# A transformer layer with attention, gated DeltaNet and routed experts: front work moved between engines and queues, unread products on TensorE, router by blocks of 128 channels

## The chip, the cores and the metric

One core of a Trainium2 chip runs the whole layer. The metric is device time in microseconds, the median of the runs shown. Times inside the kernel are microseconds from the first instruction of one profiled execution.

## The reference, cut to what matters

One layer on 1024 latent and 256 context tokens of 1024 channels, float32. RMSNorm and modulation, one input projection (2832 columns), then two groups of heads: softmax attention (8 query heads, 2 key heads) and a gated DeltaNet (4 heads of 128, scanned in both directions). One output projection, a gated residual, and experts that choose their tokens:

```
h2 = modulate(rmsnorm(x, norm2_w), sh2, sc2)
affinity = softmax(h2 @ router_w)                      # 1024 x 16
gates, idx = top_k(affinity.T, 128)                    # 128 tokens for each of 16 experts
hid = silu(xg @ w_gate) * (xg @ w_up)                  # xg = h2[idx]
x = x + g2 * scatter_add(idx, (hid @ w_down) * gates)
```

## The kernel before, in words

Every large product is done in three passes of float32r halves (high times high, low times high, high times low), so each weight matrix is split into a high part (ScalarE copy) and a low part (a subtraction). A compiler orders each engine's instructions ahead of time from the program's order and its own estimates; each engine and each DMA queue then runs its list strictly in that order. `issue_after` puts an instruction behind a named one on its engine.

*Front, about 50 to 410 us.* `in_proj` (line 503) goes over eleven groups of columns. While group i is multiplied, `weights` (413) loads and splits group i+1: the subtraction (426) is on VectorE for the first groups and on GpSimd from the seventh on. Convolved channels (`conv_head`, `conv_tail`) go to DRAM as `skT` and `sqT`. Between the tiles of the later groups, `tick` runs pieces of the DeltaNet's preparation: `dn_chunk` (798) loads keys and queries of a chunk (`kq`, two loads) and a row of cumulated decays (`grow`), subtracts the decay of each row on GpSimd (808), takes Relu (814) and Exp (815) of 512 elements on ScalarE for two or three matrices E, multiplies keys by keys and queries on TensorE (825, 827), scales the products by E on VectorE (829 to 834) and masks them on GpSimd (843). `dn_wave` (848) inverts 32x32 blocks in 62 small VectorE instructions and stores the inverse and its transpose `sT`; the transposition (869) and both stores are on ScalarE and its queue. `rope_first` prepares keys with tiles of one buffer each (`sr_raw`, `sr_sp`), loads on SyncE (1027), stores on ScalarE's queue (1029). Queries (629) and the output gate (617) leave PSUM through `zz`, a tile with two buffers, whose store (626, 636) SyncE issues.

*Middle, about 410 to 880 us.* `att_open` (1041) loads the split keys (`ksplit`, 1052, SyncE; three loads through two slots) and transposes them (1056). Twenty `dn_step`s (949) and sixteen `att_group`s (1087) alternate. Each step loads eight small blocks of the inverse (896), the matrix N, keys, values, and `kT` and `qT` separately, all on SyncE. `att_q` (1064) prepares the next two query tiles when a group has hp == 2.

*Output and routing, about 860 to 978 us.* For each of eight token tiles: `out_norm`, `out_mm` (48 products of 512 columns in two halves of the row), and `out_route` (1289): eight transposes over channels with stride 8 (1300), two copies to SBUF (1301), eight narrow products with the router's weights (1305), a copy (1308), one more product (1315); one Square over the 1024 channels (1311), the inverse root in eleven tiny VectorE instructions, the logits (1318), the exponential (1320) and the scaled row `xn` (1324) that is stored for the experts' gather. `top_out` sorts and merges the tile's affinities on VectorE with a short product between (1402). After tile 7, line 237 takes the threshold, `route` (1452 to 1487) ranks the tokens, `expert_pick` (1500) makes the indices, and the gathered rows are transposed (1526).

*Experts, about 978 us to the end.* `expert_mm` streams 144 products of 512 columns an expert; a planner (`queue`) fixes every engine's order.

Of the kernel before, what the change touches and what calls it, by code (L numbers as in the profile page):

```python
# [32 lines left out]
P = 128  # L33
D = 1024
KT = 8
# [48 lines left out]
class Layer:  # L84
# [51 lines left out]
    def build(self):  # L136
# [13 lines left out]
        self.att_open()  # L150
        self.dn_open()
# [261 lines left out]
    def weights(self, col0, n, extra=None, eng=None):  # L413
# [6 lines left out]
        for k in range(0, KT, 4):  # L420
# [5 lines left out]
            (eng or nc.vector).tensor_tensor(lo[:, k:k + 4], raw, hi[:, k:k + 4], op=ALU.subtract)  # L426
# [76 lines left out]
    def in_proj(self, first):  # L503
# [4 lines left out]
        self.skT = self.dr.tile([NT, P, DH, P], F32, name="skT")  # L508
        self.sqT = self.dr.tile([NT, P, DH, P], F32, name="sqT")
# [48 lines left out]
        for i, (nm, c0, h, extra) in enumerate(groups):  # L558
            if i + 1 < len(groups):
                W.append(self.weights(groups[i + 1][1], 256, eng=nc.gpsimd if i > 5 else nc.vector))  # L560
# [34 lines left out]
        self.close("kp")  # L595
        self.close("pp")
# [20 lines left out]
    def out_gate(self, hi, lo, h2):  # L617
        nc = self.nc
        for t in range(NLAT):
            ps = self.bank("s")  # L620
            self.token_major(ps, t + NCTX, hi, lo, 0, 256)
            th = self.wp.tile([P, 256], F32, name="zt", bufs=1)
            nc.scalar.activation(th, ps[:, :256], AF.Tanh, scale=0.5)
            z = self.wp.tile([P, 256], F32, name="zz", bufs=2)
            nc.vector.scalar_tensor_tensor(z, th, 1.0, ps[:, :256], op0=ALU.add, op1=ALU.mult)  # L625
# [3 lines left out]
    def queries(self, hi, lo, g):  # L629
        nc = self.nc  # L630
        for t in range(NLAT):
            ps = self.bank("s")
            self.token_major(ps, t + NCTX, hi, lo, 0, 256)
            q = self.wp.tile([P, 256], F32, name="zz", bufs=2)
# [37 lines left out]
    def conv_tail(self, cp, name, h, acc, b0):  # L672
# [7 lines left out]
        if name != "v":  # L680
            st = self.sqT if name == "q" else self.skT
# [21 lines left out]
    def gates(self):  # L703
# [53 lines left out]
        v.tensor_copy(tot.rearrange("p c u -> p (c u)"), ps[:, 80:160])  # L757
        self.egc, self.ekd, self.egl = new("egc", k), new("ekd", k), new("egl", k)
# [39 lines left out]
    def dn_chunk(self, pp, c):  # L798
# [4 lines left out]
        nc.sync.dma_start(kq[:, :, 0], self.skT[c])  # L803
        if lat:
            nc.sync.dma_start(kq[:, :, 1], self.sqT[c])
        gr = pp.tile([P, 8, P], F32, name="grow", bufs=2)
        nc.sync.dma_start(gr.rearrange("p u j -> p (u j)"), dram(self.sgc, c * 8 * P, [[0, P], [1, 8 * P]]))
        nc.gpsimd.tensor_tensor(gr, gr, self.gc[:, c, :, None].to_broadcast([P, 8, P]), op=ALU.subtract)
        E = {}
        for key, d, sg in (("f", 0, 1.0), ("b", 1, -1.0), ("q", 0, -1.0)):  # L810
# [3 lines left out]
            nc.scalar.activation(e, gr[:, 4 * d:4 * d + 4], AF.Relu, scale=sg)  # L814
# [33 lines left out]
    def dn_wave(self, pp, w, units, v):  # L848
        nc = self.nc
        n = 16 * len(units)  # L850
        sT = self.dr.tile([2, P, 1024], F32, name=f"sT{w}")
# [17 lines left out]
        nc.scalar.copy(Tt[:n], T[:n].rearrange("p i j -> p j i"))  # L869
        nc.scalar.dma_start(sT[0, :n], T[:n].rearrange("p i j -> p (i j)"))  # L870
        nc.scalar.dma_start(sT[1, :n], Tt[:n].rearrange("p i j -> p (i j)"))


    def dn_open(self):
        nc = self.nc
        sp = self.sp = self.open("sp")
        self.F = [[sp.tile([P, DH, P], F32, name=f"F{d}{i}") for i in range(2)] for d in range(2)]
        self.X = [[sp.tile([P, DH, 64], F32, name=f"X{d}{i}") for i in range(2)] for d in range(2)]
        for d in range(2):
            for i in range(2):  # L880
                nc.gpsimd.memset(self.F[d][i], 0.0)
                nc.gpsimd.memset(self.X[d][i], 0.0)
# [3 lines left out]
    def dn_merge(self, sp, s, d, c):  # L886
        nc = self.nc
        F, X = self.F[d][s % 2], self.X[d][s % 2]
        sT, i = self.sT[c, d]
        base = i * 16 * 1024  # L890
        of, ox = (1, 0) if d == 0 else (0, 1)
        for b in range(4):
            pr = slice(32 * b, 32 * b + 32)
            cb = 32 * (b % 2)
            for dst, o in ((F[pr, :, 32 * b:32 * b + 32], of), (X[pr, :, cb:cb + 32], ox)):
                nc.sync.dma_start(dst, dram(sT, o * P * 1024 + base + b * 1024, [[32, 32], [4096, DH], [1, 32]]))
# [880 lines left out]
```

## Time and profile before

| | us |
|---|---|
| runs shown (three) | 1550.82, 1551.98, 1552.12; median 1551.98 |
| the profiled execution's own time | 1550.66 |
| its span, first to last instruction | 1548.9 |
| TensorE busy | 1443.1 |
| VectorE / ScalarE / GpSimd busy | 1178.0 / 949.0 / 222.8 |
| mean granted clock of TensorE | 0.967 |

Outside the span lie 1.8 us. [...]

### The profile page before, as it was taken

Reading aid. Unit: us, or ns where it says so; the run is one execution under the profiler, and the core shown is the slowest. Engines: PE = TensorE matmul, PEld = TensorE weight load, DVE = VectorE, ACT = ScalarE, POOL = GpSimd, SP = SyncE. Lnnn points to the kernel's source line nnn. Section 1 sums busy time; section 2 is a strip of 40 time slices with the busy share of each in tenths; the row PEclk is TensorE's granted clock in tenths of the full one; section 3 lists DMA queues with packets and bytes.
Section 4 is the critical chain, followed back from the end, with each engine's and each line's share of the span. In section 5 each row is a group of like instructions: output and inputs, shape, how many; then the busy total and the mean of one; then the engine's idle time right before and its main releaser. Section 6 shows DMA issues by size and latency. Waiting matters only on the chain.

```text
span 1548.9 us, 25613 instructions
## 1 busy us (share of the span) xinstructions
PE 1443.1 (93%) x9416; PEld 1173.8 (76%) x9416; DVE 1178.0 (76%) x2456; ACT 949.0 (61%) x1513; POOL 222.8 (14%) x230
## 2 busy tenths in 40 slices
PE   4899998997899999999899996799999999999997
PEld 1887787886777787788577664688888888888885
DVE  2825578698678686576574588899999999999996
ACT  2815455434285544566774543688888888888884
POOL 0000003423111121111400021111111111111101
PEclk7999999997999999999999998899999999999999
DMA  9356826777734456541342575889999999999992
GB/s 356 103 187 212 287 84 180 223 237 247 224 82 146 138 176 183 143 136 53 94 149 94 181 292 211 315 300 394 382 396 394 394 387 391 399 396 384 381 371 43
DMA packets 187048, 377.27 MB, mean 244 GB/s; under 512 B 47631, under 2 KB 124187, under 8 KB 159403
## 3 DMA queue, kind: packets, MB, share of 16 engines
q1 hardware_dynamic: 176320, 339.94, 61.9%
q0 software_dynamic: 7488, 29.36, 6.3%
q10 hardware_dynamic: 3115, 6.34, 1.1%
q8 instruction: 74, 1.21, 0.3%
q14 instruction: 51, 0.42, 0.1%
HBM read 321.91 MB, written 53.68 MB: 242 GB/s over the span
## 4 chain that ended last, share of the span: by engine, by line
PE 71%; DVE 12%; DMA 8%; ACT 5%; issue 2%; POOL 1%; SPq 1%; POOLq 0%; ACTq 0%; DVEq 0%
PE ps_m L1601 32%; PE ps_t L1129 4%; PE ps_a L1112 3%; PE ps_t L1122 3%; PE ps_s L441 3%; PE ps_s L443 3%; PE ps_s L442 3%; PE ps_t L1601 2%; PE ps_d L975 1%; DMA woraw<-in_w_out 1%; DMA sz<-zz 1%; PE ps_d L296 1%; PE ps_d L981 1%; PE ps_d L1284 1%; PE ps_d L1283 1%
## 5 line engine op out<-in xcount | busy, mean ns | idle before, releaser
L1601 PE MATMUL ps_m<-ehi,xx 128*128 128x512 f32 x1024 | 259.7, 396 | 0.4 <-DVE xx L1538 0.4
L1601 DVE TENSOR_TENSOR elo<-eraw,ehi 128x2048 fp32r<-128x2048 f32 x102 | 231.3, 2288 | 20.1 <-ACT ehi L1601 19.6
L1601 ACT ACTIVATE ehi<-eraw 128x2048 fp32r<-128x2048 f32 x105 | 201.3, 1918 | 54.7 <-PE ps_m L1601 45.4
L1601 PEld LDWEIGHTS ps_m<-ehi,xx 128*128 128x128 f32 x1024 | 189.9, 189 | 38.3 <-ACT xf L1534 0.8
L1601 PE MATMUL ps_m<-elo,xx 128*128 128x512 f32 x512 | 137.4, 390 | 0.0
L1601 PE MATMUL ps_m<-ehi,hx 128*128 128x512 f32 x512 | 129.7, 395 | 0.0
L1115 DVE TENSOR_SCALAR_CACHE_REDUCE prob<-ps_a 128x416 f32<-128x416 f32 (+1 forms) x192 | 109.4, 595 | 26.0 <-PE ps_a L1112 16.2
L1601 DVE TENSOR_TENSOR elo<-fraw,ehi 128x2048 fp32r<-128x2048 f32 x51 | 115.8, 2287 | 9.1 <-ACT ehi L1601 9.0
L1112 PE MATMUL ps_a<-kts,QT 128*128 128x416 f32 (+1 forms) x384 | 109.1, 390 | 4.0 <-DVE prob L1115 3.9
L1601 ACT ACTIVATE ehi<-fraw 128x2048 fp32r<-128x2048 f32 x51 | 97.8, 1917 | 24.2 <-PE ps_m L1601 21.4
L1601 PEld LDWEIGHTS ps_m<-elo,xx 128*128 128x128 f32 x512 | 96.3, 188 | 20.5
L1123 ACT ACTIVATE PT<-ps_t 128x512 f32<-128x512 f32 (+1 forms) x192 | 93.7, 525 | 28.8 <-PE ps_t L1122 26.9
L1601 PEld LDWEIGHTS ps_m<-ehi,hx 128*128 128x128 f32 x512 | 94.0, 188 | 18.2
L1122 PE MATMUL ps_t<-consts,prob 128*128 128x128 f32 x640 | 100.2, 282 | 3.1 <-ACT PT L1123 1.7
L433 PE MATMUL ps_s<-whi,hh 128*128 128x256 f32 (+1 forms) x336 | 98.0, 293 | 3.9 <-DVE zz L625 2.1
L1745 POOL DMA_INDIRECT out_x<-ey,idx x16 | 52.0, 3252 | 342.3 <-DVE ey L1601 342.3
L1118 ACT ACTIVATE prob<-prob,mn 128x1280 f32<-128x1280 f32 x64 | 87.2, 1363 | 19.1 <-DVE mn L1117 18.4
L435 PE MATMUL ps_s<-whi,hl 128*128 128x256 f32 (+1 forms) x336 | 95.8, 289 | 0.9 <-DVE hl L410 0.9
L434 PE MATMUL ps_s<-wlo,hh 128*128 128x256 f32 (+1 forms) x336 | 95.5, 287 | 0.0
L441 PE MATMUL ps_s<-hh,whi 128*128 128x512 f32 (+1 forms) x256 | 95.1, 372 | 0.0
L443 PE MATMUL ps_s<-hh,wlo 128*128 128x512 f32 (+1 forms) x256 | 94.3, 368 | 0.0
L442 PE MATMUL ps_s<-hl,whi 128*128 128x512 f32 (+1 forms) x256 | 94.0, 367 | 0.0
(434 smaller groups left out, 3134.5 us busy)
## 6 DMA issues: line engine op xcount, KB each, us to landing
eraw<-in_w_up SPq DMA_DIRECT2D x38, 1024.0 KB, 9.4
eraw<-in_w_down SPq DMA_DIRECT2D x32, 1024.0 KB, 7.0
eraw<-in_w_gate SPq DMA_DIRECT2D x31, 1024.0 KB, 8.8
wmod<-in_w_mod SPq DMA_DIRECT2D x24, 1024.0 KB, 6.3
fraw<-in_w_down SPq DMA_DIRECT2D x21, 1024.0 KB, 7.6
fraw<-in_w_gate SPq DMA_DIRECT2D x16, 1024.0 KB, 9.8
fqraw<-in_w_gate SPq DMA_DIRECT2D x16, 1024.0 KB, 9.7
fraw<-in_w_up SPq DMA_DIRECT2D x14, 1024.0 KB, 8.4
```

The source lines that it names most:

```text
L433: self.nc.tensor.matmul(ps[:, :n], self.hh[:, k, ts], hi[:, k, a:a + n], start=st, stop=False)
L434: self.nc.tensor.matmul(ps[:, :n], self.hh[:, k, ts], lo[:, k, a:a + n], start=False, stop=False)
L435: self.nc.tensor.matmul(ps[:, :n], self.hl[:, k, ts], hi[:, k, a:a + n], start=False, stop=en)
L441: self.nc.tensor.matmul(ps[:, :n], hi[:, k, a:a + P], self.hh[:, k, ts], start=st, stop=False)
L442: self.nc.tensor.matmul(ps[:, :n], hi[:, k, a:a + P], self.hl[:, k, ts], start=False, stop=False)
L443: self.nc.tensor.matmul(ps[:, :n], lo[:, k, a:a + P], self.hh[:, k, ts], start=False, stop=en)
L1112: nc.tensor.matmul(ps[:, k0:min(k0 + 512, w)], QT[:, h, i], self.KTs[:, kv * 2 + x, ks], start=x == 0, stop=x == 1)
L1115: v.tensor_scalar(pr[:, c0:c0 + w], ps[:, :w], -1.0, 3e38, op0=ALU.mult, op1=ALU.min, accum_out=mn[:, y:y + 1])
L1118: nc.scalar.activation(pr, pr, AF.Exp, bias=mn[:, 3:4], scale=-1.0, accum_out=rs[:, a, hp, i:i + 1])
L1122: nc.tensor.transpose(pt[:, x * P:(x + 1) * P], pr[:, (k0 + x) * P:(k0 + x + 1) * P], self.ident)
L1123: nc.scalar.activation(PT[g][:, :, a, i], pt[:, :n * P].rearrange("p (x q) -> p x q", x=n), AF.Copy)
L1601: i = fn(*args, **kw)
```

## The change

It has four groups of edits. (1) **Front:** the weight split is always on VectorE; the decay of the row is added inside ScalarE's Relu, head by head (four of 128 in place of one of 512), so the GpSimd subtraction is gone; `skT` and `sqT` become one array `skq` with one load in place of two, in `dn_chunk` and in `dn_step`; `zz` has four buffers in a pool of its own and the tanh is done in place; the router's loads are issued at the first query group and its constants are made before the last gate group; the inverse and its transpose are stored from SyncE, the transposition is on VectorE; the eight block loads of a step become four. (2) **Attention's start:** the first query tile is prepared before the DeltaNet's tiles are opened, the next ones at hp == 1; `ksplit` and the first query tile are loaded from GpSimd's queue, and the third key load has a slot of its own. (3) **Router:** transposes take contiguous blocks of 128 channels (the router's weights are re-laid through DRAM), the square is taken per half row between them, and the row copy is tied behind the exponential. (4) **Unread products:** 18 products of 512 columns in bfloat16 behind tile 7's product of line 1402, and 10 behind the second `expert_pick`; nothing reads them.

```diff
@@ build, in_proj, weights
         self.att_open()
+        self.att_q(0)
         self.dn_open()
-            (eng or nc.vector).tensor_tensor(lo[:, k:k + 4], raw, hi[:, k:k + 4], op=ALU.subtract)
+            nc.vector.tensor_tensor(lo[:, k:k + 4], raw, hi[:, k:k + 4], op=ALU.subtract)
...
+                self.zp = self.open("zp")
+                self.router_loads(self.wp)
...
-                self.out_gate(hi, lo, h)
                 if h:
                     self.router_consts(self.wp)
+                self.out_gate(hi, lo, h)
@@ out_gate (queries alike)
-            z = self.wp.tile([P, 256], F32, name="zz", bufs=2)
+            z = self.zp.tile([P, 256], F32, name="zz", bufs=4)
@@ dn_chunk
-        nc.sync.dma_start(kq[:, :, 0], self.skT[c])
-        if lat:
-            nc.sync.dma_start(kq[:, :, 1], self.sqT[c])
+        nc.sync.dma_start(kq if lat else kq[:, :, 0], self.skq[c] if lat else self.skq[c, :, :, 0])
...
-        nc.gpsimd.tensor_tensor(gr, gr, self.gc[:, c, :, None].to_broadcast([P, 8, P]), op=ALU.subtract)
...
-            nc.scalar.activation(e, gr[:, 4 * d:4 * d + 4], AF.Relu, scale=sg)
+            off = self.ngc if sg > 0 else self.gc
+            for h in range(DH):
+                u = 4 * d + h
+                nc.scalar.activation(e[:, h], gr[:, u], AF.Relu, bias=off[:, c, u:u + 1], scale=sg)
@@ dn_wave
-        nc.scalar.copy(Tt[:n], T[:n].rearrange("p i j -> p j i"))
-        nc.scalar.dma_start(sT[0, :n], T[:n].rearrange("p i j -> p (i j)"))
-        nc.scalar.dma_start(sT[1, :n], Tt[:n].rearrange("p i j -> p (i j)"))
+        nc.sync.dma_start(sT[:, 0].rearrange("g (b r) -> g b r", b=4), T[:n].rearrange("p i j -> p (i j)"))
+        v.tensor_copy(Tt[:n], T[:n].rearrange("p i j -> p j i"))
+        nc.sync.dma_start(sT[:, 1].rearrange("g (b r) -> g b r", b=4), Tt[:n].rearrange("p i j -> p (i j)"))
@@ dn_merge
-            for dst, o in ((F[pr, :, 32 * b:32 * b + 32], of), (X[pr, :, cb:cb + 32], ox)):
-                nc.sync.dma_start(dst, dram(sT, o * P * 1024 + base + b * 1024, [[32, 32], [4096, DH], [1, 32]]))
+            nc.sync.dma_start(FX[32 * b:32 * b + 32, :, 32 * b:32 * b + 32], dram(sT, base + b * 1024, [[32, 32], [4096, 2 * DH], [1, 32]]))
@@ att_open, att_group
-            s = tp.tile([P, 2048], F32, name="ksplit", tag="PT4", bufs=2)[:, :512 * T]
+            s = (tw if T == 2 else tp).tile([P, 512 * T], F32, name="ksplit", tag=f"PT{T}", bufs=2)
-            nc.sync.dma_start(s, self.sks[t0:t0 + T].rearrange("t p i d -> p t i d"))
+            nc.gpsimd.dma_start(s, self.sks[t0:t0 + T].rearrange("t p i d -> p t i d"))
...
-        if hp == 2 and j < 3:
+        if hp == 1 and j < 3:
@@ out_route
-                nc.tensor.transpose(pt[:, i * P:(i + 1) * P], xv[:, 4 * g + i], self.ident)
+                nc.tensor.transpose(pt[:, i * P:(i + 1) * P], x1[:, (4 * g + i) * P:(4 * g + i + 1) * P], self.ident)
+
+            nc.scalar.activation(junk, x1[:, 512 * g:512 * g + 512], AF.Square, scale=D ** -0.5, accum_out=ss[:, g:g + 1])
...
-        nc.scalar.activation(junk, x1, AF.Square, accum_out=ss)
-        v.tensor_scalar(ss, ss, 1.0 / D, EPS, op0=ALU.mult, op1=ALU.add)
+        v.tensor_scalar(ms, ss[:, 0:1], ss[:, 1:2], EPS, op0=ALU.add, op1=ALU.add)
...
-        nc.scalar.activation(xn, x1, AF.Copy, scale=r2)
+        with self.tc.issue_after(ex.ins):
+            nc.scalar.activation(xn, x1, AF.Copy, scale=r2)
@@ top_out, experts
+            if t == NLAT - 1:
+                self.spin("d", 18, listed)
...
+    def spin(self, tag, n, behind):
+        ps = self.bank(tag)
+        with self.tc.issue_after(behind.ins):
+            for _ in range(n):
+                last = self.nc.tensor.matmul(ps, self.oneb, self.info.rearrange("p t e c -> p (t e c)")[:, :512], start=True, stop=True)
...
+        self.spin("m", 10, self.picked)
```

## Rows read from the trace of the kernel before

**Rows 1.** The profile's page: busy us, share of the span and instructions of each engine (PEld: weight loads of TensorE).

```profile
PE 1443.1 (93%) x9416; PEld 1173.8 (76%) x9416; DVE 1178.0 (76%) x2456; ACT 949.0 (61%) x1513; POOL 222.8 (14%) x230
```

**Rows 2.** The table of windows, whole core: the window, its length, then busy us (and instructions) of TensorE, its weight loads, VectorE, ScalarE and GpSimd, then TensorE's granted clock as a share of full speed, the DMA engines' busy share and GB/s.

```profile
240.00:280.00 40.00, 34.53 (x183) 29.04 (x182) 34.53 (x52) 20.28 (x36) 20.46 (x15) 0.96 0.80 233
...
320.00:360.00 40.00, 27.02 (x216) 25.73 (x214) 38.01 (x104) 15.83 (x26) 17.07 (x9) 0.84 0.72 230
...
400.00:440.00 40.00, 35.11 (x279) 31.54 (x277) 25.65 (x82) 21.94 (x45) 7.68 (x13) 0.91 0.75 203
600.00:640.00 40.00, 35.03 (x331) 30.21 (x330) 27.21 (x79) 19.72 (x43) 8.56 (x8) 0.87 0.59 176
```

**Rows 3.** What TensorE waited for between 225 and 425 us: engine, tile and line that waited, what ended the wait, us in total, times, longest.

```profile
PE ps_d L827 <- DVE Eb L834: 4.3, 1, 4.3
...
PE ps_a L1056 <- DVE rbias L1208: 2.7, 1, 2.7
PE ps_s L433 <- DVE zz L625: 2.1, 2, 1.1
PE ps_s L433 <- ACT zz L635: 1.8, 1, 1.8
```

**Rows 4.** Groups of instructions by line and shape: count, busy us, mean ns, idle before. The first is VectorE between 100 and 225 us (GpSimd free), the second the same line between 225 and 420 us.

```profile
L661 DVE SCALAR_TENSOR_TENSOR cacc<-craw,cw,cacc 128x1284 f32<-128x1284 f32 x16 | 24.9, 1556 | 0.7
...
L661 DVE SCALAR_TENSOR_TENSOR cacc<-craw,cw,cacc 128x1284 f32<-128x1284 f32 x16 | 28.3, 1769 | 0.4
```

**Rows 5.** The same view, GpSimd between 225 and 420 us; and the lines of the weight split by engine (ns min/median/max, first and last start).

```profile
L808 POOL TENSOR_TENSOR grow<-grow,g_gc 128x1024 f32<-128x1024 f32 x10 | 20.4, 2038 | 34.4 <-DMA grow<-sgc 34.4
L426 POOL TENSOR_TENSOR wlo<-wraw,whi 128x1024 fp32r<-128x1024 f32 x8 | 20.0, 2506 | 44.1 <-ACT whi L425 38.2 <-PE ps_t L690 6.0
...
L426 DVE TENSOR_TENSOR wlo<-wraw,whi x14: 1217/1222/1294, 34.8 to 210.3; 128x1024 fp32r<-128x1024 f32 x12, 128x1088 fp32r<-128x1088 f32 x2
```

**Rows 6.** ScalarE: the decay activation on 512 elements, a 128-element activation without a pointer operand (both 225 to 420 us), and one whose bias and scale are both per-partition pointers (min/median/max ns).

```profile
L814 ACT ACTIVATE Ef<-grow 128x512 f32<-128x512 f32 x10 | 6.3, 628 | 18.6 <-DVE rs_i L126 6.5 <-POOL grow L808 6.1 <-DMA sN<-Ef 3.1
L695 ACT ACTIVATE cjunk<-ps_t 128x128 bf16<-128x128 f32 x6 | 1.7, 278 | 0.2
...
L1534 ACT ACTIVATE xf<-ps_t,sh,a x4: 450/457/457, 976.9 to 979.5; 128x128 f32<-128x128 f32 x4
```

**Rows 7.** What the DMA queue of SyncE waited for between 225 and 420 us (columns as in rows 3).

```profile
SPq L769 <- DVE g_ckb L784: 20.4, 1, 20.4
SPq L626 <- DVE zz L625: 13.6, 7, 5.0
```

**Rows 8.** The largest stall, in order of time: a transfer from the chain of waits (start, us), an issue of SyncE's queue, and TensorE's next two products with the idle time before them.

```profile
339.76 8.68 DMA sks<-sr_sp
...
351.29 0.37 SPq L1027 DMA_DIRECT2D sr_raw<-skr  x1
...
356.15 2.04 PE L825 MATMUL ps_d<-kq 128*128 128x256 f32 x4 [11.18 <-issue]
361.47 2.04 PE L825 MATMUL ps_d<-kq 128*128 128x256 f32 x4 [3.27 <-DVE rs_a L130]
```

**Rows 9.** SyncE's queue before the opening of attention, in order of time (a row of two stores spans the time between them).

```profile
403.57 3.93 SPq L626 DMA_DIRECT2D sz<-zz  x2
407.59 0.39 SPq L1052 DMA_DIRECT2D ksplit<-sks  x1
```

**Rows 10.** What TensorE waited for between 880 and 985 us (columns as in rows 3).

```profile
PE ps_r L1315 <- ACT lg L1308: 1.8, 2, 1.4
PE ps_r L1305 <- ACT xT L1301: 1.5, 2, 0.9
```

**Rows 11.** Tile 7, ScalarE in order of time: square, row copy, exponential.

```profile
950.20 1.06 ACT L1311 ACTIVATE j<-xres 128x1024 bf16<-128x1024 f32 x1 [9.20 <-issue]
...
953.91 1.15 ACT L1324 ACTIVATE xn<-xres,rs_r 128x1024 f32<-128x1024 f32 x1 [0.71 <-DVE rs_r L132]
954.97 0.29 ACT L1320 ACTIVATE aff<-logit,mx 128x16 f32<-128x16 f32 x1
```

**Rows 12.** Before and at the start of the experts, windows of 5 us (columns as in rows 2).

```profile
955.00:960.00 5.00, 0.92 (x16) 0.69 (x16) 4.32 (x35) 4.06 (x5) 1.73 (x6) 0.50 0.99 410
960.00:965.00 5.00, 0.00 (x0) 0.00 (x0) 4.97 (x38) 1.91 (x1) 0.00 (x0) 0.50 1.02 428
...
980.00:985.00 5.00, 5.00 (x19) 3.96 (x17) 3.90 (x8) 1.92 (x1) 0.62 (x1) 0.77 1.02 429
```

**Rows 13.** TensorE there, in order of time, with the idle time before a group and what ended it.

```profile
958.56 0.59 PE L1402 MATMUL ps_l<-srt,consts 128*16 128x32 f32 x8 [2.19 <-DVE j1x L1347]
965.54 0.61 PE L1452 MATMUL ps_m<-consts,m 16*128 16x16 f32 x2 [6.39 <-DVE m L237]
...
972.06 0.37 PE L1500 MATMUL ps_t<-info,oh 128*128 128x5 bf16 x8 [1.55 <-DVE oh L1493]
976.21 1.97 PE L1526 MATMUL ps_t<-consts,xg 128*128 128x128 f32 x8 [3.77 <-DMA xg<-h,idx]
978.62 3.75 PE L1601 MATMUL ps_m<-ehi,xx 128*128 128x512 f32 x8 [0.43 <-DVE xx L1538]
...
983.16 2.00 PE L1601 MATMUL ps_m<-ehi,xx 128*128 128x512 f32 x8
...
985.90 1.98 PE L1601 MATMUL ps_m<-ehi,xx 128*128 128x512 f32 x8
```

More of the change, by code (lines that the diff above doesn't have):

```diff
@@ L559, in in_proj @@
             if i + 1 < len(groups):
-                W.append(self.weights(groups[i + 1][1], 256, eng=nc.gpsimd if i > 5 else nc.vector))
+                W.append(self.weights(groups[i + 1][1], 256))
             hi, lo = W.pop(0)
@@ L595, in in_proj @@
         self.close("kp")
+        self.close("zp")
         self.close("pp")
@@ L621, in out_gate @@
             self.token_major(ps, t + NCTX, hi, lo, 0, 256)
-            th = self.wp.tile([P, 256], F32, name="zt", bufs=1)
-            nc.scalar.activation(th, ps[:, :256], AF.Tanh, scale=0.5)
-            z = self.wp.tile([P, 256], F32, name="zz", bufs=2)
-            nc.vector.scalar_tensor_tensor(z, th, 1.0, ps[:, :256], op0=ALU.add, op1=ALU.mult)
+            z = self.zp.tile([P, 256], F32, name="zz", bufs=4)
+            nc.scalar.activation(z, ps[:, :256], AF.Tanh, scale=0.5)
+            nc.vector.scalar_tensor_tensor(z, z, 1.0, ps[:, :256], op0=ALU.add, op1=ALU.mult)
             nc.sync.dma_start(self.sz[t, :, h2:h2 + 2, :], z.rearrange("p (h d) -> p h d", h=2))
@@ L757, in gates @@
         v.tensor_copy(tot.rearrange("p c u -> p (c u)"), ps[:, 80:160])
+        self.ngc = new("ngc", k)
+        v.tensor_scalar(self.ngc, self.gc, -1.0, None, op0=ALU.mult)
         self.egc, self.ekd, self.egl = new("egc", k), new("ekd", k), new("egl", k)
@@ L876, in dn_open @@
         sp = self.sp = self.open("sp")
-        self.F = [[sp.tile([P, DH, P], F32, name=f"F{d}{i}") for i in range(2)] for d in range(2)]
-        self.X = [[sp.tile([P, DH, 64], F32, name=f"X{d}{i}") for i in range(2)] for d in range(2)]
+        self.FX = [[sp.tile([P, 2 * DH, P], F32, name=f"F{d}{i}") for i in range(2)] for d in range(2)]
         for d in range(2):
             for i in range(2):
-                nc.gpsimd.memset(self.F[d][i], 0.0)
-                nc.gpsimd.memset(self.X[d][i], 0.0)
+                nc.gpsimd.memset(self.FX[d][i], 0.0)
         self.so = [[self.dr.tile([P, DH, P], F32, name=f"so{d}_{t}") for t in range(NLAT)] for d in range(2)]
@@ L1189, in router_consts @@
         nc.sync.dma_start(m[:, 4], self.col(A["norm2_w"], 0))
+        rw = pool.tile([P, KT, NE], F32, name="rw")
+        nc.sync.dma_start(rw, dram(A["router_w"], 0, [[KT * NE, P], [1, KT * NE]]).rearrange("p (k e) -> p k e", k=KT))
+        self.router = m, rw
+    def router_consts(self, pool):
+        nc, k = self.nc, self.keep
+        v = nc.vector
+        m, rw = self.router
         self.sh2 = k.tile([P, KT], F32, name="sh2")
@@ L1295, in out_route @@
         xT = wo.tile([P, KT, P], F32, name="xT", bufs=1)
-        xv = x1.rearrange("p (q k) -> p k q", k=KT)
+        ss = wo.tile([P, 2], F32, name="ss2", bufs=2)
+        junk = wo.tile([P, 512], BF, name="j2", bufs=1)
         for g in range(2):
@@ L1319, in out_route @@
         v.tensor_reduce(mx[:, 0:1], lo, axis=AX.X, op=ALU.max, negate=True)
-        nc.scalar.activation(self.aff[:, t], lo, AF.Exp, bias=mx[:, 0:1], accum_out=mx[:, 1:2])
+        ex = nc.scalar.activation(self.aff[:, t], lo, AF.Exp, bias=mx[:, 0:1], accum_out=mx[:, 1:2])
         v.reciprocal(mx[:, 1:2], mx[:, 1:2])
```

66 lines of the change are left out of this document (30 added, 36 removed).

## The prediction

> **What bounds the kernel now.** The page comes first: TensorE is busy 1443.1 us of a span of 1548.9 and every other engine is far below it [rows 1], so time comes back where TensorE stands still or runs at its lower clock ahead of the experts; behind 978 us it streams products. The table of windows shows where: idle 5.5 us in 240 to 280, 13.0 in 320 to 360, 4.9 in 400 to 440, 5.0 in 600 to 640, with clocks of 0.84 to 0.96 [rows 2]. [...] The waits of TensorE and of SyncE's queue then say what ended each gap. In the front it is three things: VectorE late with the matrices E, the two-buffered zz, and SyncE's queue standing behind a wait [rows 3, 7, 8]. In the tail it is a chain of small VectorE and ScalarE instructions, behind which TensorE starts the experts cold [rows 10 to 13].
>
> **The change part by part.** The sum goes against the profiled execution's own 1550.66 us; the median of the runs shown, 1551.98, stands 1.3 above it and gets the same difference.
>
> *GpSimd's front work.* 20.4 us of row subtraction and 20.0 of weight split leave GpSimd [rows 5]. While GpSimd runs, VectorE is slow: line 661 takes 1556 ns a piece with GpSimd free and 1769 on average beside it, 3.4 us over 16 [rows 4]. The split comes back to VectorE as 8 pieces of 1.22 us, 9.8 us [rows 5], and the transposition of the inverse comes as well. So VectorE's total hardly falls; what falls is the path to E, which loses one subtraction of 2.04 us and a turn in GpSimd's list. The wait that this path ends is 4.3 us [rows 3]; two split pieces may stand before the products there (2.4 us). Bounds: -4.3 less the clock behind it (0.96 in that window, 3.2 us at half speed, 1.6 lost), so -5.9, to +2.4 if VectorE is simply later. I take **-3.5**, near the lower end, as the row waited for is E itself.
>
> *Relu head by head.* One activation of 512 elements is 628 ns [rows 6]. Four of 128 are between 4 x 0.278 = 1.11 us (no pointer operand) and 4 x 0.455 = 1.82 (two pointers) [rows 6]; the new one has one pointer. 28 matrices E make +13.5 to +33 us of ScalarE, which is busy 15.8 to 21.9 of 40 us there [rows 2], so most of it lies beside other work. [...] Exposed I take **+1.5** (0 to +15).
>
> *zz with four buffers.* TensorE waited 2.1 + 1.8 us for a bank that waited for zz, and SyncE's list stood 13.6 us for the gate's part of it alone [rows 3, 7]. Two more buffers cover a store of some 4 us. **-3.9** (0 to -3.9); late next is ScalarE's evacuation itself.
>
> *Attention's start.* The first transposition waited 2.7 us for the router's bias [rows 3], which is now made a group of columns earlier. The key load stood behind two output-gate stores for 3.9 us on SyncE [rows 9] and now goes on GpSimd's list, free there. [...] I take **-4.5** for waits and clock together (0 to -6.6, 2.7 + 3.9; the near end if the load is late anyway). [...]
>
> *The large stall.* From 344.98 to 361.47 TensorE does four products: SyncE's list stood at the load of sr_raw until 351.29, since VectorE waited for sr_sp, whose store took 8.68 us; kq came behind it [rows 8]. The change leaves sr_raw, sr_sp and that store as they are. Two waits, 11.18 + 3.27, and the slow clock (0.84, 12.8 us at half speed, mostly idle) make -17.5 the far end; the near end is 0. kq is one load instead of two, VectorE is disturbed less, and the second wait ended at a VectorE line. **-3.0**.
>
> *Stores of the inverse on SyncE, steps with fewer loads, att_q earlier.* ScalarE loses a copy a wave; each step issues five loads less. But the stores wait for VectorE's last instruction of a wave, and behind them in SyncE's list stand the next step's loads. The gap in 600 to 640 (5.0 us, clock 0.87, some 10 us at half speed) falls where att_q(2) and two steps meet; it can go or move. Bounds -10 to +40 (a rival below); I take **-1.0**.
>
> *Router.* TensorE waited 1.8 + 1.5 us for the copies of the logits and of the transposed row [rows 10]. The first half of a row can be transposed and squared before the second is there, and the Square of 1.06 us no longer stands before both copies [rows 11]. Two accumulator reads instead of one add some 0.2 us. **-2.5** (0 to -5). For tile 7 the exponential waited 0.94 us behind the row copy (953.91 to 954.97) [rows 11], but VectorE is busy 4.3 and 5.0 of each 5 us behind it [rows 12], so only its 0.7 us of idle can be won: **-0.7**. The router's weights through DRAM are ready hundreds of us early: 0.
>
> *Unread products.* TensorE is at half clock from 955 to about 982.3 (0.77 over 980 to 985 means 2.3 us slow) [rows 12]. The first twelve expert products took 983.16 - 978.62 = 4.54 us, the next twelve 985.90 - 983.16 = 2.74 [rows 13]; so a product is 0.23 us at full and 0.46 at half speed. 18 of them need 4.1 to 8.2 us; the room between lines 1402 and 1452 is 965.54 - 959.15 = 6.4 us [rows 13]. From 978.62 the first group of eight (3.75 us) went by before the clock rose [rows 12, 13]; eight slow and ten fast ones take 6.0 us: they just fit. The second ten (2.3 to 4.6 us) lie in the 3.7 us between 972.43 and the gathered rows at 976.21 [rows 13]. Won: 1.8 us on the first products and about 1.0 on ranks and transposes at half speed. **-2.8** (-3.5 to +1.8 if the block stays slow and delays line 1452).
>
> Sum: -3.5 + 1.5 - 3.9 - 4.5 - 3.0 - 1.0 - 2.5 - 0.7 - 2.8 = -20.4 us; 1550.66 becomes 1530.3, and the median 1531.6.
>
> **The rivals.** *The front gives it back.* The lists are in order, and SyncE, ScalarE and VectorE take on each other's work; if the front's gaps only move, zz, the router and the unread products remain: -3.9 - 2.5 - 0.7 - 2.8 = -9.9, 1542. For it: VectorE is busy 38.0 of 40 us in 320 to 360 [rows 2]. Against: 40 us of GpSimd work are gone.
>
> *The large stall goes too.* With another order of SyncE's list kq is loaded before sr_raw, and -3.0 becomes -17.5: 1517. For it: the order is made anew. Against: the same loads with the same single buffers.
>
> *Slower: SyncE held at the inverse's stores.* SyncE's list has stood 20.4 us for a VectorE result at line 769 [rows 7]. If the two later waves hold it as long in the middle of the scan, the steps' loads come late and TensorE, in order, stands: 2 x 20.4 = +40.8 on the sum, 1572. It decides from about 10 us a wave, where the gain is eaten. Against: twenty steps with five loads less leave that list slack, and attention groups lie between.
>
> *The unread products don't raise the clock.* Then -2.8 is 0 to +1.8, some 1535, inside the forecast's own range.
>
> **How the numbers follow.** Forecast 0.50 (with its own range, 1523 to 1539), gives back 0.23, stall gone too 0.16, held stores 0.11, of which 0.08 end slower and 0.03 near no change. Chances: faster 0.89, same 0.03, slower 0.08, by 0.2%, 3.1 us, about what a measurement of this kernel can tell from no change. The range 1511 to 1549 takes the first three cases with their spread and leaves out the held stores.
>
> **What would show it.** Right: no wait of line 433 for zz; no wait for the bias at line 1056; line 661 near 1556 ns in the front; the clock at full level at the first expert products, and twelve of them in 2.7 us; line 1452 not later behind line 1402 than 6.4 us. The stall at line 825 shows by its idle time which of the first three cases it is. Wrong: TensorE idle behind 420 us at lines 896 to 1009 while SyncE's list waits for the transposed inverse; the second row of products delaying the transposes of line 1526; or ScalarE full between 240 and 400 us, with products waiting for E.

## The result: 10 us faster, half of the forecast

| | median us | runs | range | ratio to before, 95% interval |
|---|---|---|---|---|
| before | 1552.05 | 10 | 1549.85 to 1559.29 | 1 |
| after | 1542.9 | 10 | 1539.5 to 1547.53 | 0.9933 [0.9915, 0.9951] |

The profiled execution took 1540.66 us, span 1538.9, against 1550.66 and 1548.9 before. Forecast were 1531.6 and a gain of 20.4. The milestones of the profiles (starts, us) say where the forecast parts from the run; the last column is an experiment told below.

| milestone | before | after | difference | early merge |
|---|---|---|---|---|
| end of the projection's products | 408.1 | 389.8 | -18.3 | 392.5 |
| first transposition of keys | 411.2 | 399.2 | -12.0 | 400.6 |
| first product of attention | 422.0 | 410.9 | -11.1 | 412.5 |
| last attention group copied out | 871.3 | 854.8 | -16.4 | 855.1 |
| tile 7: copy of the logits | 952.9 | 937.8 | -15.1 | 938.3 |
| tile 7: copy of its lists | 959.2 | 946.6 | -12.6 | 944.9 |
| reduction to the threshold | 965.2 | 957.0 | -8.2 | 950.5 |
| first expert product | 978.6 | 970.3 | -8.3 | 963.3 |
| 13th expert product | 983.2 | 973.2 | -10.0 | 966.1 |
| end of the span | 1548.9 | 1538.9 | -10.0 | 1532.0 |

So in these two profiles the front won 16.4 us where its terms summed to 14.4. From there to the threshold 8.2 were lost where 3.2 were to be won, and the unread products won 1.8. The 16.4 comes from one execution of each kernel: in seven profiles with this front the last attention group is copied out between 854.5 and 862.4 us, a gain of 8.9 to 16.7.

### The profile page after: what moved, and what is told of

Read it like the earlier page. It is cut to its first block, busy times and chain, and to the rows that moved or that the text cites. A ratio compares the mean times of both kernels' runs of the same rounds, so it can differ in the third digit from the quotient of the medians.

```text
span 1538.9 us, 25604 instructions
## 1 busy us (share of the span) xinstructions
PE 1448.0 (94%) x9442; PEld 1178.5 (77%) x9444; DVE 1170.9 (76%) x2468; ACT 961.1 (62%) x1610; POOL 187.6 (12%) x214
## 4 chain that ended last, share of the span: by engine, by line
PE 59%; DVE 7%; DMA 4%; ACT 3%; issue 2%; SPq 1%; POOL 0%; POOLq 0%; DVEq 0%; ACTq 0%
PE ps_m L1620 32%; PE ps_a L1110 4%; PE ps_t L1120 4%; PE ps_t L1127 4%; PE ps_t L1620 2%; PE ps_d L975 1%; PE ps_d L981 1%; PE ps_d L1290 1%; PE ps_d L1291 1%; PE ps_d L1289 1%; PE ps_d L1009 1%; PE ps_d L990 1%; DMA woraw<-in_w_out 1%; PE ps_d L1003 1%; PE ps_d L936 1%
## 5 line engine op out<-in xcount | busy, mean ns | idle before, releaser
L1620 DVE TENSOR_TENSOR elo<-eraw,ehi 128x2048 fp32r<-128x2048 f32 x102 | 231.1, 2286 | 18.6 <-ACT ehi L1620 17.6
L1620 PEld LDWEIGHTS ps_m<-elo,xx 128*128 128x128 f32 x512 | 96.1, 188 | 20.4
L1620 PEld LDWEIGHTS ps_m<-ehi,hx 128*128 128x128 f32 x512 | 93.9, 188 | 18.2
```

The costliest lines, as they stand in the source:

```text
L1620: i = fn(*args, **kw)
```

## The profile after

The page (columns as in [rows 1]), then the windows of [rows 2]: the idle 13 us of 320 to 360 are gone, 13.3 new ones stand in 360 to 400, and the gap of 600 to 640 is closed.

```profile
PE 1448.0 (94%) x9442; PEld 1178.5 (77%) x9444; DVE 1170.9 (76%) x2468; ACT 961.1 (62%) x1610; POOL 187.6 (12%) x214
```

```profile
240.00:280.00 40.00, 38.88 (x215) 32.71 (x214) 34.33 (x58) 32.32 (x83) 4.41 (x9) 1.00 0.89 277
320.00:360.00 40.00, 37.95 (x293) 36.86 (x293) 39.31 (x149) 26.51 (x71) 3.85 (x6) 1.00 0.88 293
360.00:400.00 40.00, 26.74 (x205) 26.23 (x204) 25.37 (x77) 9.49 (x20) 9.55 (x13) 0.90 0.73 241
400.00:440.00 40.00, 36.79 (x317) 30.32 (x315) 28.14 (x87) 27.02 (x53) 7.25 (x8) 0.93 0.53 119
600.00:640.00 40.00, 39.76 (x415) 33.72 (x415) 22.30 (x73) 20.16 (x47) 6.25 (x6) 1.00 0.51 145
```

TensorE's waits between 225 and 425 us, as in [rows 3]. The waits for Eb and for the bias are gone; zz still costs 4.1, and the keys' load is the new longest.

```profile
PE ps_a L1056 <- DMA ksplit<-sks: 9.5, 2, 9.1
PE ps_s L434 <- DVE zz L627: 4.1, 1, 4.1
PE ps_d L829 <- DVE rs_a L131: 2.0, 2, 1.7
PE ps_t L1080 <- DMA sr_sp<-sqs: 2.0, 1, 2.0
```

Groups by line and shape between 225 and 420 us: the convolution's line of [rows 4], the weight split of [rows 5], now on VectorE, and the Relu of [rows 6], now by heads.

```profile
L663 DVE SCALAR_TENSOR_TENSOR cacc<-craw,cw,cacc 128x1284 f32<-128x1284 f32 x16 | 24.8, 1551 | 0.3
...
L427 DVE TENSOR_TENSOR wlo<-wraw,whi 128x1024 fp32r<-128x1024 f32 x8 | 9.7, 1218 | 1.3 <-PE ps_t L692 0.7 <-ACT whi L426 0.6
...
L818 ACT ACTIVATE Eb<-grow,g_gc 128x128 f32<-128x128 f32 x40 | 13.5, 391 | 0.0
```

The end, TensorE and then windows of 5 us, against [rows 12, 13]: the first twelve expert products take 2.84 us instead of 4.54, but 11.5 us lie between line 1411 (1402 before) and line 1471 (1452), where 7.0 lay before. The 18 unread products (1 + 16 in the rows, one record missing) end at 952.9, and TensorE then stands for 4.5 us.

```profile
945.91 0.61 PE L1411 MATMUL ps_l<-srt,consts 128*16 128x32 f32 x8 [2.10 <-DVE srt L1344]
946.45 0.61 PE L1437 MATMUL ps_d<-info,oneb 128*128 128x512 bf16 x1
947.27 5.67 PE L1437 MATMUL ps_d<-info,oneb 128*128 128x512 bf16 x16 [0.22 <-issue]
957.43 0.36 PE L1471 MATMUL ps_m<-consts,m 16*128 16x16 f32 x2 [4.50 <-DVE m L238]
...
964.30 4.05 PE L1437 MATMUL ps_m<-info,oneb 128*128 128x512 bf16 x9 [0.24 <-issue]
968.14 1.21 PE L1545 MATMUL ps_t<-consts,xg 128*128 128x128 f32 x8
970.33 2.10 PE L1620 MATMUL ps_m<-ehi,xx 128*128 128x512 f32 x8 [0.97 <-DVE xx L1557]
```

```profile
945.00:950.00 5.00, 3.87 (x16) 1.78 (x18) 5.00 (x38) 4.42 (x3) 0.57 (x1) 0.50 1.00 419
950.00:955.00 5.00, 2.94 (x11) 0.94 (x8) 4.76 (x32) 0.00 (x0) 0.00 (x0) 0.86 0.89 371
955.00:960.00 5.00, 2.19 (x27) 2.12 (x27) 3.46 (x16) 0.00 (x0) 0.00 (x0) 0.82 0.00 2
960.00:965.00 5.00, 1.52 (x21) 0.94 (x20) 3.84 (x8) 0.00 (x0) 1.97 (x2) 0.50 0.00 0
965.00:970.00 5.00, 4.35 (x16) 2.11 (x14) 4.57 (x5) 0.81 (x2) 4.14 (x4) 0.65 0.70 206
```

What fills these 11.5 us is seen by cutting windows from the copy of tile 7's lists to the reduction to the threshold (fourth column VectorE, with its number of instructions), before, after and in the early-merge kernel below:

```profile
959.19:965.22 6.03, 0.00 (x0) 0.00 (x0) 5.96 (x43) 2.48 (x2) 0.00 (x0) 0.50 1.01 426
```

```profile
946.55:957.01 10.46, 6.17 (x17) 2.17 (x17) 10.01 (x66) 2.87 (x2) 0.00 (x0) 0.77 0.75 316
```

```profile
944.87:950.48 5.61, 4.99 (x17) 1.88 (x17) 5.09 (x28) 2.75 (x2) 0.00 (x0) 0.78 1.02 428
```

VectorE is all but full in all three (99, 96 and 91% busy); it has 43, 66 or 28 instructions left. In the kernel after, merges of earlier tiles still stand there. Between the logits of tiles 4 and 7 VectorE had stood idle instead, 10.2 of 47.6 us against 4.4 of 46.8 before:

```profile
906.13:952.93 46.80, 43.20 (x276) 31.40 (x276) 42.41 (x251) 16.60 (x40) 9.58 (x22) 1.00 0.44 169
```

```profile
890.20:937.83 47.63, 44.92 (x276) 32.16 (x276) 37.47 (x202) 17.33 (x46) 9.19 (x22) 0.96 0.37 148
```

## The experiments

Groups of kernels ran on different chips, each beside the kernel before, so kernels are compared by that ratio: 0.001 is 1.55 us, and the intervals reach 0.002 to 0.003 to each side, so that two kernels are told apart from a difference of about 0.004, or 6 us, on. Smaller differences rest on the profiles alone, of one execution each. The front's share varies there too: in seven profiles with the same front (the kernel after, the first four experiments on the tail, the front alone, and the second key load first, whose front differs in that order alone) the projection ends between 389.1 and 396.2 us.

**The tail.** *Without the unread products*

```
-                self.spin("d", 18, listed)
-        self.spin("m", 10, self.picked)
```

> The changed kernel without both rows of unread products; nothing else differs, and VectorE's list is the same. Theory A (the tail is later because of the order of VectorE's list, in which 65 instead of 42 instructions stand between the copy of tile 7's lists and the reduction to the threshold): that stretch stays at some 10.9 us, the first twelve expert products take about 4.5 us again instead of 2.7, so some 1.5 to 2.5 us more than the changed kernel, about 1545. Theory B (the unread products themselves hold the tail up): the stretch falls to about 6.4 us, and the time is some 2 to 4 us less than the changed kernel's, about 1540.

Measured: 0.9954 [0.9933, 0.9975], so 3.3 us more than the change by the ratios, though the intervals overlap. From the copy of tile 7's lists to the threshold ("lists to threshold" below) it is 10.46 us, as with the unread products; the twelve expert products take 4.19. Theory B falls: the unread products don't hold the tail up.

*The first row of them only*

```
-        self.spin("m", 10, self.picked)
```

> The changed kernel with the 18 unread products behind tile 7's lists but without the ten behind the second pick. Theory A: the 18 end some 4.5 us before the threshold's product, so TensorE is at half clock again at the ranks, and the ten alone raise the clock for the experts; time as without both, about 1545, the first twelve expert products about 4.5 us. Rival: the 18 are what keeps the clock; then about 1543, as the changed kernel, and twelve expert products in about 2.7 us.

Measured: 0.9958 [0.994, 0.9976]; twelve expert products 3.96 us. The 18 alone give nothing that can be told from none; it takes the ten to raise the clock for the experts, as A has it. All fourteen profiles (before, after and the twelve experiments) agree: in the seven with the ten the clock is at its upper level (1.00; the lower is 0.50) 1.7 to 3.4 us ahead of the first expert product, and the first twelve take 2.84 to 2.86 us; in the seven without them it rises 1.3 to 4.3 us behind that product, and the twelve take 3.48 to 4.83. The ten without the 18 were not run.

*The old router under the new front*

```
-                nc.tensor.transpose(..., x1[:, (4 * g + i) * P:(4 * g + i + 1) * P], self.ident)
+                nc.tensor.transpose(..., xv[:, 4 * g + i], self.ident)
...
-        with self.tc.issue_after(ex.ins):
```

> The changed kernel with the router of before (strided transposes, one square of the whole row, row copy not tied). In VectorE's list 28 instead of 65 instructions then stand between the copy of tile 7's lists and the reduction to the threshold. Theory A: that stretch falls from 10.9 to some 6 us while each tile's logits come 1 to 3 us later; the time is 1 to 3 us less than the changed kernel's, about 1541. Rival C (the router's edit saves what the forecast put there, and the list's order costs nothing because VectorE has the same work in all): 2.5 to 3.2 us more than the changed kernel, about 1546.

Measured: 0.991 [0.9884, 0.9936], 3.6 us less than the change; lists to threshold 5.61. Rival C falls in the profile, where the 5.61 leave no doubt; the times' intervals overlap.

*The merge put early*: the router's edit kept, one priority altered.

```
-        with self.tc.high_priority(-LP):
+        with self.tc.high_priority(0):
             self.top_out(3, at3)
```

> The changed kernel with one priority altered: the merge of the lists of the first four tiles is no longer put 200 places back. The work is the same; in VectorE's list 28 instead of 65 instructions stand between the copy of tile 7's lists and the reduction to the threshold, and the merge can fill VectorE's idle time between 908 and 935. Theory A: 4 to 5 us less than the changed kernel, about 1538. Rival C (VectorE's total work sets the end, its order does not matter): within 1 us of the changed kernel, about 1543.

Measured: 1535.46 us, 0.9891 [0.9871, 0.9912], 6.5 us less than the change by the ratios, with intervals that don't overlap, and 6.98 by the spans. The work is the same; the merge of the first four tiles starts at 909.90 (first row) instead of 934.24 (second row, the kernel after):

```profile
909.90 0.41 DVE L1377 TENSOR_TENSOR m_3x<-lists 16x256 f32<-16x256 f32 x1
```

```profile
934.24 0.41 DVE L1377 TENSOR_TENSOR m_3x<-lists 16x256 f32<-16x256 f32 x1 [1.95 <-ACT lists L1427]
```

The order of VectorE's list is shown as the tail's cause. The place of that merge follows the router: in the seven profiles with the new router and the old priority it starts 10.7 us behind tile 6's copy of the logits, and lists to threshold take 10.46 or 10.47 us; in the other seven it starts ahead of that copy, and they take 5.61 to 6.03.

With the merge early, threshold to 13th expert product takes 15.63 us against 17.94 before and 16.16 after. Over the fourteen profiles it is 15.6 to 16.3 with the ten unread products and 17.0 to 18.2 without, so they are worth 1.6 us on average; the pair's 2.3 is at the upper end.

*The front alone*: old router, no unread products (the two edits above together).

> The changed kernel with the router of before and without unread products, so the front's edits alone. Theory A: the stretch from the copy of tile 7's lists to the threshold is some 5.6 us as with the old router and the unread products, and the first twelve expert products take some 4.2 to 4.5 us; 1.5 to 2.5 us more than that kernel, about 1541, so faster than the whole change. Rival C (router and unread products are worth what the forecast said): some 6 us more than the changed kernel, about 1549.

Measured: 1537.22, 0.9907 [0.9881, 0.9932]; lists to threshold 5.61, twelve expert products 4.83. The front alone is not slower than the whole change, as A has it; C's +6 is excluded. The old router with the unread products had 0.991: the 1.9 us that the profiles give them there can't be seen in the times.

*The new router alone, on the kernel before*

```
-                nc.tensor.transpose(..., xv[:, 4 * g + i], self.ident)
+                nc.tensor.transpose(..., x1[:, (4 * g + i) * P:(4 * g + i + 1) * P], self.ident)
...
+        with self.tc.issue_after(ex.ins):
```

> The kernel before with the new router alone (transposes, squares and weights by blocks of 128 channels, row copy tied behind the exponential). In VectorE's list 65 instead of 42 instructions then stand between the copy of tile 7's lists and the reduction to the threshold. Theory A: that stretch grows from 6.0 to some 10.5 us; what the router saves per tile is given back, and the time is 1 to 5 us more than before, about 1556. Rival C (the forecast's 2.5 and 0.7 us): about 3 us less than before, 1550.

Measured: 1563.2, 1.007 [1.0043, 1.0097]: 10.9 us slower than the kernel before, more than A's 5. Lists to threshold 10.46 (+4.4); tile 7's logits to its lists 8.73 against 6.26; last attention group to tile 7's logits 85.2 against 81.7. The router's edit by itself, with the merge in its old place, is a loss.

**The front.** *GpSimd at work again*: row subtraction, whole Relu and the last splits as before, in the changed kernel.

```
+        nc.gpsimd.tensor_tensor(gr, gr, self.gc[:, c, :, None].to_broadcast([P, 8, P]), op=ALU.subtract)
...
-                nc.scalar.activation(e[:, h], gr[:, u], AF.Relu, bias=off[:, c, u:u + 1], scale=sg)
+            nc.scalar.activation(e, gr[:, 4 * d:4 * d + 4], AF.Relu, scale=sg)
...
+                W.append(self.weights(groups[i + 1][1], 256, eng=nc.gpsimd if i > 5 else nc.vector))
```

> The changed kernel with the row subtraction and the last weight splits on GpSimd again, and the Relu whole. In VectorE's list the first instruction that empties the fifth chunk's products stands 86 places behind the first step of the inverse. Theory P: VectorE's instructions beside GpSimd's split are long again, chunk products wait 4 to 8 us more, and the time is 5 to 9 us more than the changed kernel's, about 1550. Rival Q: with the early place in the list the stall stays away and ScalarE is relieved of some 20 us; within 2 us of the changed kernel, about 1544.

Measured: 1567.3, 1.0087 [1.0058, 1.0117], 24 us more than the change, where P had 5 to 9; the projection ends at 408.2, 18.4 later. The waits for Eb (5.7) and the large stall (11.37) are back. GpSimd, VectorE and TensorE there, in order of time:

```profile
346.15 2.35 POOL L427 TENSOR_TENSOR wlo<-wraw,whi 128x1024 fp32r<-128x1024 f32 x1 [12.45 <-ACT whi L426]
348.46 1.89 POOL L810 TENSOR_TENSOR grow<-grow,g_gc 128x1024 f32<-128x1024 f32 x1
350.31 2.35 POOL L427 TENSOR_TENSOR wlo<-wraw,whi 128x1024 fp32r<-128x1024 f32 x1
352.62 1.91 POOL L810 TENSOR_TENSOR grow<-grow,g_gc 128x1024 f32<-128x1024 f32 x1
```

```profile
345.51 0.25 DVE L869 TENSOR_TENSOR T<-T,Ttmp 128x87 f32<-128x87 f32 x1
345.68 0.41 DVE L831 TENSOR_TENSOR Qb<-ps_d,Eb 128x256 f32<-128x256 f32 x1
...
346.73 1.84 DVE L869 TENSOR_TENSOR T<-T,Ttmp 128x60 f32<-128x60 f32 x1
348.50 1.88 DVE L480 TENSOR_SCALAR sr_s<-sr_s 128x8 f32<-128x8 f32 x1
350.30 0.41 DVE L832 TENSOR_TENSOR Eq<-ps_d,Eq 128x256 f32<-128x256 f32 x1
350.63 2.09 DVE L867 TENSOR_TENSOR Ttmp<-L,T 128x31 f32<-128x31 f32 x1
352.64 1.91 DVE L125 TENSOR_SCALAR rs_i<-sr_s 128x8 int32<-128x8 int32 x1
...
356.66 0.34 DVE L836 SCALAR_TENSOR_TENSOR Eb<-ps_d,g_bp,Eb 128x128 f32<-128x128 f32 x1
```

```profile
338.10 1.89 PE L827 MATMUL ps_d<-kq 128*128 128x256 f32 x8
357.10 2.04 PE L827 MATMUL ps_d<-kq 128*128 128x256 f32 x4 [11.37 <-issue]
```

For 8.4 us VectorE gets one small instruction done for each of GpSimd's: four that need 0.2 us take 1.84 to 2.09, and each ends when a GpSimd instruction ends. The instruction that reads a bank of products passes in 0.41. Behind them stand the last readers of the bank (356.66 + 0.34 = 357.00), and TensorE goes on at 357.10. So P's mechanism is shown, though its size was far too small, and Q falls: the early place in the list alone does not keep the stall away. An estimate for the whole front takes every VectorE instruction between 225 and 410 us that lasted over 0.15 us longer than the median of its shape with GpSimd idle: 18.9 us are lost so in the kernel before, 24.1 here, 9.8 in the next run, 3.4 in the changed kernel; the projection ends at 408.1, 408.2, 401.1 and 389.8. Three edits are taken back here at once, and their shares are not separated.

*The split alone taken from GpSimd, on the kernel before*

```
-                W.append(self.weights(groups[i + 1][1], 256, eng=nc.gpsimd if i > 5 else nc.vector))
+                W.append(self.weights(groups[i + 1][1], 256))
```

> The kernel before with the weight split on VectorE throughout, and nothing else. In VectorE's list the first instruction that empties the fifth chunk's products stands 116 places behind the first step of the inverse (115 before, 81 in the changed kernel). Theory P (the large stall ends when VectorE has emptied the two banks of the chunk's products, and beside GpSimd's split VectorE's small instructions take up to 2 us instead of 0.2 to 0.7): the stall falls from 14.5 to 5 to 9 us and the time by 4 to 9 us, to about 1546. Rival Q (the place in VectorE's list decides alone): the stall stays over 11 us and the time within 3 us of before, about 1552.

Measured: 1.001 [0.9992, 1.0029], no gain; the stall falls to 9.03 + 0.29 us and the projection ends at 401.1, 7.0 earlier, both nearer to P, while the time is Q's. But the first product of attention starts at 441.7 (422.0 before): another order of the lists puts steps of the scan first, and the gain is gone by there. Half of GpSimd's work given up is worth nothing here.

*Three buffers for zz, on the kernel before*

```
-            z = self.wp.tile([P, 256], F32, name="zz", bufs=2)
+            z = self.wp.tile([P, 256], F32, name="zz", bufs=3)
```

(and the same for the queries)

> The kernel before with three buffers for zz instead of two, and nothing else. In SyncE's list both loads of kq that stood behind the third load of sr_raw then stand ahead of it or one place behind. Theory D (the large stall was a matter of the order of that list): of the idle 11.2 and 3.3 us ahead of the chunk's products at line 825 at most some 4 are left, and the time is 8 to 12 us less than before, about 1542. Rival E (the stall hangs on the 8.7 us store of the split keys, which stays): only the waits for zz go, 2 to 4 us, about 1549.

Measured: 1561.53, 1.0051 [1.0034, 1.0069]: slower, and neither theory had that. The stall is 14.79 us. kq has two buffers, so its loads and the ten chunks' products pair off in order; it is the eighth chunk that stalls, and its loads, the first two rows, were issued 28 us before TensorE goes on (the pair that the edit moved ahead of sr_raw, issued at 346.29, is the ninth chunk's). TensorE follows the last reader of its bank (360.57 + 0.59 = 361.16):

```profile
332.76 0.53 SPq L803 DMA_DIRECT2D kq<-skT  x1
333.34 0.72 SPq L805 DMA_DIRECT2D kq<-sqT  x1
```

```profile
360.57 0.59 DVE L834 SCALAR_TENSOR_TENSOR Eb<-ps_d,g_bp,Eb 128x128 f32<-128x128 f32 x2
```

```profile
361.27 2.04 PE L825 MATMUL ps_d<-kq 128*128 128x256 f32 x4 [14.79 <-issue]
```

D falls, and with it the reading of [rows 8]. The time is lost behind the projection: attention's first product comes at 451.9.

*Two buffers for zz in the changed kernel*

```
-            z = self.zp.tile([P, 256], F32, name="zz", bufs=4)
+            z = self.zp.tile([P, 256], F32, name="zz", bufs=2)
```

(and the same for the queries and the router's constants)

> The changed kernel with two buffers for zz instead of four; in SyncE's list the last load of kq falls behind the third load of sr_raw again. Theory D: a wait of 5 to 8 us ahead of the chunk's products at line 829 comes back, in part hidden since the attention's start waits for the keys' load anyway; 2 to 7 us more than the changed kernel, about 1547. Rival F (GpSimd's work given up is what took the stall away): no such wait; at most 2 us more, about 1544.

Measured: 0.9957 [0.9934, 0.9981], 3.7 us more than the change, within the intervals. Waits for zz of 2.49 and a stall of 2.98 come back, not 5 to 8; the projection ends at 394.8, inside the spread of its kind. Inconclusive on the time; most of the stall does not hang on zz.

*The second key load first, merge early*

```
+        for t0, T, s in (parts[1], parts[0], parts[2]):
             nc.gpsimd.dma_start(s, self.sks[t0:t0 + T].rearrange("t p i d -> p t i d"))
```

> The changed kernel with the early merge, and with the second of the three loads of the split keys put first: its buffer does not lie over the tile from which the split queries are stored. Theory G (the 9.1 us ahead of the first transposition are a wait for that memory, and then for 3.5 MB in one go): the load starts some 15 us earlier, TensorE waits at most 4 us there, and the time is 4 to 6 us less than with the early merge alone, about 1530. Rival H (the transfer itself bounds the start, or the wait moves on to the queries' split): less than 1.5 us, about 1535.

Measured: 1534.44, 0.9892 [0.9867, 0.9916], as with the early merge alone; the wait is 7.53 against 7.82. The loads were issued at 390.27, 0.9 us behind the projection's last product: the first one was still held there, so G's early start did not come about and it was not put to the test. This version and the early merge alone can't be told apart; they are the fastest run.

*Keys and first queries on SyncE's queue again*

```
-            nc.gpsimd.dma_start(s, self.sks[t0:t0 + T]...)
+            nc.sync.dma_start(s, self.sks[t0:t0 + T]...)
```

(and the same for the queries)

> The changed kernel with the loads of the split keys and of the first split queries on SyncE's queue again; VectorE's list is the same. Theory M (the forecast's: it is the wait ahead of a load in its list that counts): behind the gate's stores and the scan's loads they start later, TensorE waits longer for the first transposition, 2 to 4 us more than the changed kernel, about 1546. Rival N (another issuer saves issue time alone, and the load waits for the memory under it in either list): within 1 us, about 1543.

Measured: 1552.07, 1.0003 [0.9985, 1.0021], 11 us more than the change, with intervals that don't overlap; but at attention's start nothing is lost: the load is issued at 390.59 (390.55 after), and the first transposition comes at 396.7 (399.2 after). M's place is wrong, N's time is wrong. In its profiled execution, which lies below its median (span 1544.2), TensorE idles 7.7 us between 500 and 600 against 2.3; what the lists change there stays open.

## Why the forecast was half right

The time fell inside the stated range with half of the gain that was forecast, and part of that is luck: the front's sum, 14.4 us, lies near what the profiles show, but of its terms one was far too small, two did not come and one misread its cause. Nor do the parts add up: put back alone, GpSimd's work costs 24 us and the key loads' queue 11, more than the whole front won. Of the signs that the forecast named, no wait for the bias, line 661 (663 after) near 1556 ns, the clock up at the first expert product and a short first dozen came; no wait for zz and at most 6.4 us between lines 1402 and 1452 did not.

*GpSimd's front work* (-3.5): mis-sized, and the step that failed in the front. Taken back together with the Relu it costs 24 us. The forecast priced GpSimd's presence by a mean, 1769 against 1556 ns [rows 4]; what counts is that small instructions of VectorE last until one of GpSimd's has ended (1.84 to 2.09 us for 0.2 in that run), and that the products' banks are emptied behind them. The kernel before shows it as well, in three instructions at the stall that otherwise take 0.17, 0.69 and 0.17 us, while a reduction (355.11) passes beside GpSimd's split in its usual 0.69:

```profile
344.67 1.89 DVE L132 SCALAR_TENSOR_TENSOR rs_r<-rs_a,rs_r 128x8 f32<-128x8 f32 x1
...
348.53 1.65 DVE L488 TENSOR_TENSOR sr_sp<-sr_raw,kcs 128x512 f32<-128x512 f32 x1 [0.66 <-DMA sks<-sr_sp]
...
355.11 0.69 DVE L478 TENSOR_REDUCE sr_s<-sr_b 128x8 f32<-128x512 f32 x1 [0.45 <-ACT sr_b L476]
355.71 0.34 DVE L834 SCALAR_TENSOR_TENSOR Eb<-ps_d,g_bp,Eb 128x128 f32<-128x128 f32 x1
...
357.16 2.06 DVE L125 TENSOR_SCALAR rs_i<-sr_s 128x8 int32<-128x8 int32 x1
```

The rows here and in that run part by form. Beside GpSimd's instructions two TENSOR_TENSOR with both inputs in SBUF and two TENSOR_SCALAR take 1.84 to 2.09 us, where the same shapes take 0.16 to 0.22 with GpSimd idle (the kernel before, 342.88 to 343.95); the one that reads a product's bank takes 0.41, the reduction 0.69. Why the forms differ was not shown. No sentence of the forecast weighed it.

*The large stall* (-3.0, or -17.5 in the second rival): gone, 1.74 us are left of 14.45. Its cause was misread. [rows 8] put SyncE's load of kq behind sr_raw, and that was taken for the cause; but that load, issued at 352.30, is the next chunk's. The stalled chunk's own load was issued 22 us before TensorE went on:

```profile
333.79 0.53 SPq L803 DMA_DIRECT2D kq<-skT  x1
```

TensorE waited for the banks of the chunk before. Their last readers on VectorE ended at 355.71 + 0.34 = 356.05 and at 361.32, and TensorE went on at 356.15 and 361.47. "Issue" behind an idle time named no releaser, and the forecast supplied one. VectorE was late for two reasons: some 5.4 of the 14.45 us were lost beside GpSimd, an estimate from the three long rows above and a fourth at 355.97 (0.94 for 0.16 us), and the rest is key preparation and steps of the inverse that its list puts ahead of the readers. Neither is enough alone: 9.3 us stay without the split, 12.0 with the readers' early place and GpSimd at work.

*Relu head by head* (+1.5): the price of one, 391 to 394 ns, lies between the forecast's bounds of 278 and 455 [rows 6]. No run shows the 15 us at which the term's range ends; measured, ScalarE spends 38.0 us in place of 17.6 (28 of 628 ns), 20.4 more, and TensorE does not wait for it among the waits above; what the edit costs in the time was not measured apart.

*zz with four buffers* (-3.9): wrong; 4.1 us are left, now for VectorE, which evacuates two chunks first. *Attention's start* (-4.5): the wait for the bias is gone, but 9.1 + 2.0 us of loads came in its place, since the first key load is issued only 0.5 us behind the projection's end (5.3 ahead of it before, at 403.11) and takes 8.6 us to land:

```profile
390.55 2.21 POOL L1052 DMA_DIRECT2D ksplit<-sks  x3 [14.18 <-DMA sz<-zz]
```

The profile names the gate's store as what held its issue; the split queries' store, issued at 384.12, is the other candidate, and no run settles it. From the projection's end to attention's first product 21.1 us pass, 13.9 before. The queue made no difference to the issue: 390.55 from GpSimd's, 390.59 from SyncE's. So the 3.9 us behind the gate's stores [rows 9], on which the term rested, were not won by the queue. By the time the queue is worth 11 us all the same, at a place that stays open. No run shows the share of the clock in the -4.5: between the projection's end and attention's first product the clock is 0.76 before (408 to 422) and 0.76 after (390 to 411).

*Steps and stores* (-1.0): from attention's first product to the last group 443.9 us against 449.2, in the profiles of the same front 442.6 to 451.8, so the gain is not clear; the gap of 600 to 640 is closed, and the held stores did not come (the rival with SyncE held at the inverse's stores: no wait of TensorE above 1.1 us at the scan's lines).

*Router* (-2.5) and *tile 7* (-0.7): the wrong sign, +8.2 together. [rows 10, 11] gave waits of which the edit does remove a part, but [rows 12] already said that VectorE bounds the tail, and the edit put VectorE's merges behind it. Tile 7's exponential waited 4.34 us for VectorE's maximum, so tying the row copy won nothing:

```profile
942.44 0.31 ACT L1328 ACTIVATE aff<-logit,mx 128x16 f32<-128x16 f32 x1 [4.34 <-DVE mx L1327]
```

Even with the merge early the router's gain does not show: from the last attention group to the threshold 93.6 and 95.4 us (the last with the early merge alone), against 92.7 and 94.0 with the old router under the same front.

*Unread products* (-2.8): right in kind, 1.8 in this pair of profiles and 1.6 on average. The second ten are what counts; the 18 ended 4.5 us too soon because the tail had grown.

The rival "the front gives it back" had the time, 1542, and not the mechanism: the front kept its gain, the router gave it back.

## What to carry to other kernels

Before pricing an edit on an engine that is full, ask what stands behind it in that engine's list: the same work in another order was worth 6.5 us here, more than the 3.2 forecast for the edit that caused it. The stalls whose releaser the profile did not name ended here at somebody's last read; so compare a stall's end with the end of every engine's instruction on the same tile before blaming a transfer, and check that the transfer is the stalled product's own. And an engine's interference is read from the longest of its neighbour's small instructions (here 1.84 to 2.09 us for 0.2), not from the mean of its large ones (1769 for 1556 ns).

## What was not expected of the hardware

Four VectorE instructions of 8 to 60 elements took 1.84 to 2.09 us, each until the GpSimd instruction beside it ended. And the clock rose within the 18 unread products (0.50 in 945 to 950, 0.86 in 950 to 955) and was at its lower level (0.50) again in 960 to 965, after TensorE had stood for 4.5 us and then run only short products; within the ten it rose once more (0.65 in 965 to 970, 1.00 from 970 on).
